# End of an FFN: splits of the embedding projection behind the last FFN tile, and half of that projection ahead of the norm's transposes

## Chip, core and metric

The kernel runs on one core of one Trainium2 chip. The metric is the device time of one execution in microseconds (us).

## What is computed

Two blocks in a row on 256 tokens of width 1024, in float32. The first block has an RWKV and a retention mixer and then a gated FFN with a short convolution; the second has a Mamba-style mixer, attention, and, behind each of these, a "per-layer embedding". The change sits where the first block's FFN ends and the second block begins. Cut to that, the reference is:

```python
def conv_ffn(h, w_up, conv_w, conv_b, w_down):
    u = h @ w_up
    ...
    u = sum(up[:, i:i + T] * conv_w[i] for i in range(CONV_WIDTH)) + conv_b
    gate, val = jnp.split(u, 2, axis=-1)
    return (jax.nn.gelu(gate, approximate=True) * val) @ w_down
...
    f = conv_ffn(rms_norm(h, norm_ffn_pre[l]), ffn_w_up[l], ffn_conv_w[l], ffn_conv_b[l], ffn_w_down[l])
    h = h + rms_norm(f, norm_ffn_post[l])
...
def mamba2_mixer(h, norm_w, in_w, ...):
    u = rms_norm_2(h, norm_w)
    zxbcdt = u @ in_w
...
def per_layer_embedding(h, p_i, norm_w, gate_w, proj_w):
    g = jax.nn.sigmoid((rms_norm_2(h, norm_w) @ gate_w).astype(jnp.float32))
    return (g * (p_i @ proj_w).astype(jnp.float32)).astype(h.dtype)
```

`p_i @ proj_w` doesn't depend on `h`. The kernel computes it early, once at each end of the FFN (index 0 ahead of it, index 1 behind it), and parks the result in DRAM (`ppd`) until the gates need it.

## The kernel before

Tokens lie in two halves of 128 (t = 0, 1). Every large product is done with three matmuls: each operand is split into a rounded part "hi" and a rest "lo", and hi*hi, hi*lo and lo*hi are summed in PSUM (`mm3`, `gemm_a` at line 273). The split (line 251) is one copy on ScalarE (hi, line 252) and one subtraction on VectorE (lo, line 253).

Weights come through `Stream.next` (line 218): SyncE issues a load of 512 KB into one of three `raw` buffers (line 230), then the chunk is split into buffers of a tag: `w`, `l`, `e` or `d`. A raw buffer is free when both halves of its split are done. Stream tiles are `whi/wlo`, `lhi/llo`, `ehi/elo`, `dhi/dlo` in the rows.

The FFN loop has 22 tiles of 128 features. For tile f TensorE computes gate and value (48 matmuls), then ScalarE and VectorE run the convolution (lines 980 and 983), the tanh form of the GELU (1002 to 1006) and the split of the result into `fah` and `fal`. The down projection of a tile follows two tiles later; for the last 7 tiles it is put off: the weights are split and kept, and `down_late` (833) does these products, 84 matmuls for both token halves, behind the last up projection. For t = 0 it takes five tiles of half 0, then two of half 1, then the last two of half 0; for t = 1 the other five of half 1. The sums stand in four `sm` banks.

Behind each half `post_norm_T` (927) follows: mean square (ScalarE Square at 921, GpSimd power at 294), the residual sum, a second mean square, the scaling (940), eight TensorE transposes (283) and the split of the transposed rows into `xTh`, `xTl`. They feed `gate_block` (1048), the z gate of the next mixer, whose weights are the four first chunks of `w_z` with tag `l`; it does half 0 and then half 1, 24 matmuls each.

`Proj` (296) is the embedding projection: its constructor loads and splits `pT` (256 KB) and two chunks of `w_proj` with tag `e`; `run(t, o)` does two groups of 6 matmuls (512 columns each), copies both to one `xs` buffer of 1024 columns (line 311, two such buffers, shared with the norms and the z gate) and stores it with one DMA (312).

A scheduler lays out the queue of each engine from the traced order and from when operands are ready by its own estimate of times; each engine then works through its queue in order. `tc.issue_after(ins)` puts every instruction traced inside the block on the engine of `ins` behind `ins` in that engine's queue. It adds no semaphore.

Of the kernel before, what the change touches and what calls it, by code (L numbers as in the profile page):

```python
# [15 lines left out]
AF = mybir.ActivationFunctionType  # L16
# [4 lines left out]
P = 128  # L21
T = 256
# [99 lines left out]
def tile_block(ctx: ExitStack, tc: tile.TileContext, io):  # L122
    nc = tc.nc
    V, S, G, PE = nc.vector, nc.scalar, nc.gpsimd, nc.tensor
    mult, add, sub = ALU.mult, ALU.add, ALU.subtract

    def pool(name, stack=ctx, **kw):
        return stack.enter_context(tc.tile_pool(name=name, bufs=1, reuse_waits="tile", **kw))
# [27 lines left out]
    def tl(pl, shape, tag, bufs=1, dt=F32):  # L156
        return pl.tile(shape, dt, tag=tag, name=tag, bufs=bufs)

    def mm():
        return tl(qp, [P, 512], "mm", 4)  # L160

    def sm():
        return tl(qp, [P, 512], "sm", 4)

    dp = pool("scratch", space=bass.MemoryType.DRAM)
    ppd = tl(dp, [4, P, D], "ppd")
# [84 lines left out]
    def split(hi, lo, src, eng=None):  # L251
        first = S.activation(out=hi, in_=src, func=AF.Copy)  # L252
        last_split[:] = first.ins, (eng or V).tensor_tensor(out=lo, in0=src, in1=hi.bitcast(F32), op=sub).ins  # L253

    def mm3(out, sh, sl, mh, ml, start, stop):
        PE.matmul(out, sh, mh, start=start, stop=False)  # L256
        PE.matmul(out, sh, ml, start=False, stop=False)  # L257
        return PE.matmul(out, sl, mh, start=False, stop=stop).ins  # L258

    def gemm_b(out, w, xT, nk=KD, off=0, start=True, stop=True, k0=0):  # L260

        for k in range(nk):
            c = slice(off + k * P, off + (k + 1) * P)
            mm3(out, w[0][:, c], w[1][:, c], xT[0][:, k0 + k, :], xT[1][:, k0 + k, :],
                start and k == 0, stop and k == nk - 1)
# [7 lines left out]
    def gemm_a(out, w, xT, t, k, off, start, stop, n=512):  # L273

        tk, c = slice(t * P, (t + 1) * P), slice(off, off + n)
        return mm3(out, xT[0][:, k, tk], xT[1][:, k, tk], w[0][:, c], w[1][:, c], start, stop)

    def transposes(src, n, xT, t, k0=0, ps_=None):

        for j in range(0, n, 4):  # L280
            ps = (ps_ or sm)().rearrange("p (a l) -> p a l", a=4)
            for i in range(4):
                last = PE.transpose(ps[:, i, :], src[:, (j + i) * P:(j + i + 1) * P], ident)  # L283
            d = (slice(None), slice(k0 + j, k0 + j + 4), slice(t * P, (t + 1) * P))
            split(xT[0][d], xT[1][d], ps)
        return last.ins

    last_split = []
# [7 lines left out]
    class Proj:  # L296
# [5 lines left out]
            st = Stream(io["w_proj"][i:i + 1], (tag,))  # L302
            self.ws = [st.next(), st.next()]

        def run(self, t, o):
            for b in range(2):
                ps = mm()
                c = slice(b * 512, (b + 1) * 512)
                for k in range(2):
                    gemm_a(ps, self.ws[k], self.px, t, k, b * 512, k == 0, k == 1)  # L310
                S.activation(out=o[:, c], in_=ps, func=AF.Copy)
            nc.sync.dma_start(out=ppd[2 * self.i + t], in_=o)


    ph = ExitStack()
# [5 lines left out]
    def b4(shape=(P, 1024)):  # L321
        return tl(p1, list(shape), "b4", 3)

    xT = (tl(p1, [P, KD, T], "xTh", 1, F32R), tl(p1, [P, KD, T], "xTl", 1, F32R))
# [8 lines left out]
    made = G.affine_select(out=ident, in_=ident, pattern=[[-1, P]], compare_op=ALU.is_ge, fill=0.0, base=0,  # L333
                           channel_multiplier=1).ins
# [8 lines left out]
    for t in range(2):  # L343
# [15 lines left out]
        for b in range(2):  # L359
            c = slice(b * 512, (b + 1) * 512)  # L360
# [436 lines left out]
    def halves(ps):  # L797
        return ps[:, 0:T], ps[:, T:2 * T]
# [57 lines left out]
    acc = None  # L856
    late = []
    pend = None
    for f in range(KD + 1):
# [24 lines left out]
        if pend is not None:  # L884
            k, x = pend
            if acc is None:
                acc = [[sm(), sm()], [sm(), sm()]]
# [13 lines left out]
    def rows(src, n=D):  # L901
        r = tl(late_pool, [P, D], "row", 2)[:, :n]
        nc.gpsimd.dma_start(out=r, in_=src.partition_broadcast(P))
        return r

    def xs_t():
        return tl(late_pool, [P, D], "xs", 2)

    def new_xT():
        return tl(late_pool, [P, KD, T], "xTh2", 1, F32R), tl(late_pool, [P, KD, T], "xTl2", 1, F32R)  # L910

    def halved(v):
        return [v[:, 0:512], v[:, 512:1024]]
# [3 lines left out]
    def mean_square(srcs, tag):  # L917

        ms = small([P, 2], tag)
        for b in range(2):  # L920
            S.activation(out=junk[b], in_=srcs[b], func=AF.Square, scale=1.0 / 32.0, accum_out=ms[:, b:b + 1])
        r = small([P, 1], tag + "r")
        V.tensor_scalar(out=r, in0=ms[:, 0:1], scalar1=ms[:, 1:2], scalar2=RMS_EPS, op0=add, op1=add)
        rsqrt(r, r, None)
        return r

    def post_norm_T(acc, gpost, gpre, xT, t):

        xs, h = halved(xs_t()), halved(h_t[t])
        gpost, gpre = halved(gpost), halved(gpre)  # L930
        r = mean_square(acc[t], "msa")
        for b in range(2):
            V.tensor_tensor(out=xs[b], in0=acc[t][b], in1=gpost[b], op=mult)
        for b in range(2):
            V.scalar_tensor_tensor(out=h[b], in0=xs[b], scalar=r, in1=h[b], op0=mult, op1=add)
        r = mean_square(h, "msb")
        for b in range(2):
            V.tensor_tensor(out=xs[b], in0=h[b], in1=gpre[b], op=mult)
        for b in range(2):
            scaled = V.tensor_scalar(out=xs[b], in0=xs[b], scalar1=r, scalar2=None, op0=mult)  # L940
            last = transposes(xs[b], 4, xT, t, 4 * b)
        return scaled.ins, last
# [19 lines left out]
    p2 = pool("p2", ph)  # L962
    wtags["e"] = (pool("p2e", ph), 3)
    wtags["d"] = (pool("p2d", ph), 4)
    proj = Proj(0, "e")
    xT = new_xT()
    gpost, gpre = rows(io["norms"][1]), rows(io["norms"][2])
    after = [post_norm_T(acc, gpost, gpre, xT, t) for t in range(2)]
    proj.run(0, xs_t())
    with tc.issue_after(after[0][1]):  # L970
        proj.run(1, xs_t())
    with tc.issue_after(opened):
        V.tensor_scalar(out=PR("fcw").rearrange("p (i f) -> p i f", i=3)[:, :, NF:], in0=PR("fcw").rearrange("p (i f) -> p i f", i=3)[:, :, NF:],
                        scalar1=0.5, scalar2=None, op0=mult)
# [2 lines left out]
    def conv(ps, c, wname, bname, ntap, nf, i):  # L977

        wv, bv = PR(wname), PR(bname)
        S.activation(out=c, in_=ps, func=AF.Identity, scale=wv[:, (ntap - 1) * nf + i:(ntap - 1) * nf + i + 1], bias=bv[:, i:i + 1])  # L980
        for d in range(1, ntap):
            j = (ntap - 1 - d) * nf + i
            V.scalar_tensor_tensor(out=c[:, d:], in0=ps[:, :T - d], scalar=wv[:, j:j + 1], in1=c[:, d:], op0=mult, op1=add)  # L983

    w_up, w_dn = Stream(io["w_up"], ("w", "w", "w", "e", "e", "e")), Stream(io["w_down"], ("l",) * 18 + ("d",) * 4)
    acc = [[sm(), sm()], [sm(), sm()]]
# [4 lines left out]
    for f in range(NF + LAG2):  # L991
        if f < NF:
            ps = mm()
            pg_, pv_ = halves(ps)
            for g_ in (pg_, pv_):
                gemm_b(g_, first.pop(0) if first else w_up.next(), xT)
            c = tl(p2, [P, 2, T], "fc", 3)
            conv(pg_, c[:, 0, :], "fcw", "fcb", 3, 2 * NF, f)
            conv(pv_, c[:, 1, :], "fcw", "fcb", 3, 2 * NF, NF + f)
            g_, v_ = c[:, 0, :], c[:, 1, :]  # L1000
            q_ = tl(p2, [P, T], "fq", 3)
            S.activation(out=q_, in_=g_, func=AF.Square, scale=math.sqrt(0.044715))
            V.scalar_tensor_tensor(out=q_, in0=q_, scalar=1.0, in1=g_, op0=add, op1=mult)
            S.activation(out=q_, in_=q_, func=AF.Tanh, scale=math.sqrt(2.0 / math.pi))
            V.scalar_tensor_tensor(out=g_, in0=q_, scalar=1.0, in1=g_, op0=add, op1=mult)
            V.tensor_tensor(out=g_, in0=g_, in1=v_, op=mult)
            a_ = tl(p2, [P, T], "fah", LATE2 + LAG2 + 1, F32R), tl(p2, [P, T], "fal", LATE2 + LAG2 + 1, F32R)
            split(a_[0], a_[1], g_)
        if f >= LAG2:
            k, x = f - LAG2, pend[f - LAG2]  # L1010
            w = w_dn.next()
            if k < NF - LATE2:
                down(acc, w, x, k, k == 0, False)
            else:
                late.append((w, x, False))
        if f < NF:
            pend.append(a_)
    proj = Proj(1, "e")


    xT = new_xT()
    gpost, gpre = rows(io["norms"][3]), rows(io["norms"][4])
    for t in range(2):
        down_late(acc, late, t, LT2, LT2T)
        post_norm_T(acc, gpost, gpre, xT, t)
    for t in range(2):
        proj.run(t, xs_t())
    ph.close()

    ph = ExitStack()  # L1030
# [33 lines left out]
    ps = mm()  # L1064
# [38 lines left out]
    ps = sm()  # L1103
# [35 lines left out]
    for c in range(2):  # L1139
        tk = slice(c * P, (c + 1) * P)  # L1140
        ps = sm()
# [6 lines left out]
    ps = sm()  # L1148
# [71 lines left out]
    acc = None  # L1220
# [17 lines left out]
    acc = [[mm(), mm()], [mm(), mm()]]  # L1238
# [5 lines left out]
    xT, g_ple = new_xT(), rows(io["norms"][5])  # L1244
# [41 lines left out]
    gate, xT = Gate(0, xT), new_xT2()  # L1286
# [99 lines left out]
    for t in range(2):  # L1386
        last = block(wkv, kvo[t], t)
# [3 lines left out]
        last = block(wq0, qo[t], t)  # L1391
# [225 lines left out]
```

## Times and profile before

| | us |
|---|---|
| median of 3 runs | 905.34 (902.51 to 908.39) |
| profiled execution | 906.97 |
| its span | 905.3 |
| TensorE busy | 863.9 (95%) |
| VectorE busy | 655.6 (72%) |
| ScalarE busy | 515.3 (57%) |
| GpSimd busy | 59.6 (7%) |

The span runs from the first to the last instruction; the profiled execution's time is 1.67 us longer. All start times below count from the start of the span. PE is TensorE, DVE VectorE, ACT ScalarE, POOL GpSimd and SP SyncE. The mean granted TensorE clock of the execution is 0.992 of full speed.

### The profile page before, as it was taken

The page shows a single profiled execution, that of the slowest core. Times are in us where ns is not written, and L with a number is a line of the kernel's source. Part 1 is how long each engine was busy: PE and PEld are TensorE (multiplying, and loading weights), DVE is VectorE, ACT ScalarE, POOL GpSimd, SP SyncE. Part 2 cuts the span into 40 slices and gives each one's busy share as a digit, 9 for nine tenths or more (in the row PEclk, how much of TensorE's full clock was granted, in tenths as well). Part 3 has the DMA queues.
Part 4 walks back from the last instruction along what each step waited for, and adds up shares of the span by engine and source line. Part 5 has one row for each costly group of instructions (what it writes and reads, how often), then busy time and mean ns, then how long its engine had stood idle before and what let it go on. Part 6 is the DMA issues. An engine that isn't in the chain of part 4 may idle for free.

```text
span 905.3 us, 15879 instructions
## 1 busy us (share of the span) xinstructions
PE 863.9 (95%) x6226; PEld 754.9 (83%) x6226; DVE 655.6 (72%) x1138; ACT 515.3 (57%) x917; POOL 59.6 (7%) x76
## 2 busy tenths in 40 slices
PE   9999999999999999999998999998999998899997
PEld 6788788789999799999997799887888777778776
DVE  7778856874665878888888767987774587757564
ACT  6555533454553666656666557677674465565652
POOL 2000000100000100000000102011000010101000
PEclk9999999999999999999999999999999999999999
DMA  8432442234765676655654627644343655432341
GB/s 279 145 131 97 135 132 71 96 115 140 241 202 175 182 246 230 221 173 183 206 190 153 228 92 242 202 167 163 119 161 95 198 174 165 155 124 95 115 139 48
DMA packets 42252, 145.48 MB, mean 161 GB/s; under 512 B 4993, under 2 KB 5569, under 8 KB 42178
## 3 DMA queue, kind: packets, MB, share of 16 engines
q1 hardware_dynamic: 41312, 141.32, 47.1%
q0 software_dynamic: 864, 3.15, 1.3%
q8 instruction: 49, 0.80, 0.4%
q14 instruction: 25, 0.20, 0.1%
q10 hardware_dynamic: 2, 0.00, 0.0%
HBM read 141.28 MB, written 3.18 MB: 160 GB/s over the span
## 4 chain that ended last, share of the span: by engine, by line
PE 42%; DMA 19%; DVE 15%; issue 14%; ACT 9%; POOL 2%; POOLq 0%; SPq 0%; ACTq 0%; DVEq 0%
PE mm L258 9%; PE mm L256 9%; PE mm L257 9%; DMA raw<-in_w_down 7%; DVE wlo L253 3%; DMA raw<-in_w_up 3%; PE sm L596 2%; ACT lhi L252 2%; ACT whi L252 2%; DMA raw<-in_w_ai 2%; PE sm L283 2%; DVE llo L253 2%; DVE elo L253 1%; DMA raw<-in_w_br 1%; PE sm L1198 1%
## 5 line engine op out<-in xcount | busy, mean ns | idle before, releaser
L252 ACT ACTIVATE whi<-raw 128x1024 fp32r<-128x1024 f32 (+1 forms) x131 | 134.4, 1030 | 111.6 <-PE mm L257 36.1
L253 DVE TENSOR_TENSOR wlo<-raw,whi 128x1024 fp32r<-128x1024 f32 (+1 forms) x130 | 153.8, 1188 | 58.7 <-ACT whi L252 57.8
L256 PE MATMUL mm<-xTh,whi 128*128 128x256 f32 x616 | 177.3, 288 | 0.2 <-ACT xTh L252 0.2
L257 PE MATMUL mm<-xTl,whi 128*128 128x256 f32 x616 | 176.2, 286 | 0.3 <-DVE xTl L253 0.3
L258 PE MATMUL mm<-xTh,wlo 128*128 128x256 f32 x616 | 175.9, 286 | 0.4 <-DVE wlo L253 0.4
L257 PEld LDWEIGHTS mm<-xTl,whi 128*128 128x128 f32 x616 | 119.1, 193 | 2.4 <-issue 0.7
L256 PEld LDWEIGHTS mm<-xTh,whi 128*128 128x128 f32 x616 | 118.9, 193 | 2.4 <-ACT xTh L252 0.5
L258 PEld LDWEIGHTS mm<-xTh,wlo 128*128 128x128 f32 x616 | 118.9, 193 | 1.2 <-DVE wlo L253 0.9
L253 DVE TENSOR_TENSOR llo<-raw,lhi 128x1024 fp32r<-128x1024 f32 x46 | 56.1, 1221 | 18.4 <-ACT lhi L252 17.9
L256 PE MATMUL mm<-whi,xTh 128*128 128x512 f32 x168 | 68.9, 410 | 0.0
L258 PE MATMUL mm<-whi,xTl 128*128 128x512 f32 x168 | 67.7, 403 | 0.0
L252 ACT ACTIVATE lhi<-raw 128x1024 fp32r<-128x1024 f32 x46 | 48.6, 1059 | 32.8 <-DMA raw<-in_w_down 13.3
L257 PE MATMUL mm<-wlo,xTh 128*128 128x512 f32 x168 | 67.1, 400 | 0.0
L256 PE MATMUL mm<-lhi,xTh 128*128 128x512 f32 (+1 forms) x156 | 61.2, 392 | 1.9 <-DVE cv L983 1.9
L257 PE MATMUL mm<-llo,xTh 128*128 128x512 f32 (+1 forms) x156 | 60.7, 389 | 0.0
L258 PE MATMUL mm<-lhi,xTl 128*128 128x512 f32 (+1 forms) x156 | 59.8, 384 | 0.0
L983 DVE SCALAR_TENSOR_TENSOR fc<-mm,par,fc 128x255 f32<-128x255 f32 x88 | 41.9, 478 | 7.8 <-ACT fc L980 7.3
L258 PE MATMUL mm<-xTh,elo 128*128 128x256 f32 x168 | 47.6, 283 | 0.0
L257 PE MATMUL mm<-xTl,ehi 128*128 128x256 f32 x168 | 47.6, 283 | 0.0
L256 PE MATMUL mm<-xTh,ehi 128*128 128x256 f32 x168 | 47.5, 283 | 0.0
L983 DVE SCALAR_TENSOR_TENSOR cv<-mm,par,cv 128x255 f32<-128x255 f32 (+2 forms) x72 | 34.2, 475 | 5.8 <-ACT cv L980 5.2
L258 PEld LDWEIGHTS mm<-whi,xTl 128*128 128x128 f32 x168 | 32.0, 191 | 6.8 <-DVE xTl L253 0.2
(468 smaller groups left out, 1977.4 us busy)
## 6 DMA issues: line engine op xcount, KB each, us to landing
raw<-in_w_up SPq DMA_DIRECT2D x44, 512.0 KB, 3.9
raw<-in_w_xbc SPq DMA_DIRECT2D x25, 512.0 KB, 4.3
raw<-in_w_ret SPq DMA_DIRECT2D x24, 512.0 KB, 3.7
raw<-in_w_down SPq DMA_DIRECT2D x22, 512.0 KB, 4.4
raw<-in_w_gate SPq DMA_DIRECT2D x16, 512.0 KB, 3.4
raw<-in_w_z SPq DMA_DIRECT2D x16, 512.0 KB, 4.2
raw<-in_w_so SPq DMA_DIRECT2D x16, 512.0 KB, 3.8
raw<-in_w_pg SPq DMA_DIRECT2D x16, 512.0 KB, 4.2
```

The costliest lines, as they stand in the source:

```text
L252: first = S.activation(out=hi, in_=src, func=AF.Copy)
L253: last_split[:] = first.ins, (eng or V).tensor_tensor(out=lo, in0=src, in1=hi.bitcast(F32), op=sub).ins
L256: PE.matmul(out, sh, mh, start=start, stop=False)
L257: PE.matmul(out, sh, ml, start=False, stop=False)
L258: return PE.matmul(out, sl, mh, start=False, stop=stop).ins
L283: last = PE.transpose(ps[:, i, :], src[:, (j + i) * P:(j + i + 1) * P], ident)
L596: PE.matmul(fv(px)[u, f, :], lhsT(f, x), rhs[u, f, :], start=True, stop=True)
L983: V.scalar_tensor_tensor(out=c[:, d:], in0=ps[:, :T - d], scalar=wv[:, j:j + 1], in1=c[:, d:], op0=mult, op1=add)
L1198: PE.matmul(py[:, i * 64:(i + 1) * 64], sg[:, i, :], x[:, i * 64:(i + 1) * 64], start=False, stop=i % 2 == 1)
```

## The change

`Proj.run` copies each group of 512 columns into a buffer of its own, one of the three `fc` buffers that the FFN tiles use for the convolution, stores it with a DMA of its own, and returns its last matmul. This holds at both ends of the FFN. Behind the FFN, the splits of `pT` and `w_proj` are queued behind both instructions of the last FFN tile's split (`made`). Then half 0's transposes are queued behind `proj.run(0)`, `proj.run(1)` behind those transposes, and half 1's norm is traced last.

```diff
-        def run(self, t, o):
+        def run(self, t):
             for b in range(2):
-                ps = mm()
-                c = slice(b * 512, (b + 1) * 512)
+                ps, o = mm(), tl(p2, [P, 2, T], "fc", 3).rearrange("p a l -> p (a l)")
                 for k in range(2):
-                    gemm_a(ps, self.ws[k], self.px, t, k, b * 512, k == 0, k == 1)
-                S.activation(out=o[:, c], in_=ps, func=AF.Copy)
-            nc.sync.dma_start(out=ppd[2 * self.i + t], in_=o)
+                    last = gemm_a(ps, self.ws[k], self.px, t, k, b * 512, k == 0, k == 1)
+                S.activation(out=o, in_=ps, func=AF.Copy)
+                nc.sync.dma_start(out=ppd[2 * self.i + t, :, b * 512:(b + 1) * 512], in_=o)
+            return last
...
-    proj.run(0, xs_t())
+    proj.run(0)
     with tc.issue_after(after[0][1]):
-        proj.run(1, xs_t())
+        proj.run(1)
...
             split(a_[0], a_[1], g_)
+            made = list(last_split)
...
-    proj = Proj(1, "e")
+
+    with tc.issue_after(made[0]), tc.issue_after(made[1]):
+        proj = Proj(1, "e")
...
     for t in range(2):
         down_late(acc, late, t, LT2, LT2T)
-        post_norm_T(acc, gpost, gpre, xT, t)
-    for t in range(2):
-        proj.run(t, xs_t())
+    with tc.issue_after(proj.run(0)):
+        turned = post_norm_T(acc, gpost, gpre, xT, 0)[1]
+    with tc.issue_after(turned):
+        proj.run(1)
+    post_norm_T(acc, gpost, gpre, xT, 1)
     ph.close()
```

## Rows read from the trace of the kernel before

**Rows 1.** The page, busy time of each engine and its share of the span.

```profile
PE 863.9 (95%) x6226; PEld 754.9 (83%) x6226; DVE 655.6 (72%) x1138; ACT 515.3 (57%) x917; POOL 59.6 (7%) x76
```

**Rows 2.** Timeline of TensorE: start us, us, engine, line, operation, tiles, [idle before <-releaser].

```profile
480.76 0.40 PE L256 MATMUL sm<-lhi,fah 128*128 128x512 f32 x1
...
490.08 0.39 PE L258 MATMUL sm<-lhi,fal 128*128 128x512 f32 x1
491.48 0.50 PE L256 MATMUL sm<-dhi,fah 128*128 128x512 f32 x1 [1.01 <-ACT fah L252]
...
492.83 0.40 PE L258 MATMUL sm<-dhi,fal 128*128 128x512 f32 x1
494.56 0.50 PE L256 MATMUL sm<-dhi,fah 128*128 128x512 f32 x1 [1.33 <-ACT fah L252]
...
495.84 0.39 PE L258 MATMUL sm<-dhi,fal 128*128 128x512 f32 x1
...
501.75 0.39 PE L257 MATMUL sm<-dlo,fah 128*128 128x512 f32 x1
504.19 1.09 PE L283 MATMUL sm<-cst,xs 128*128 128x128 f32 x8 [2.05 <-DVE xs L940]
...
506.05 0.40 PE L256 MATMUL mm<-ehi 128*128 128x512 f32 x1
...
511.50 0.39 PE L256 MATMUL mm<-lhi,xTh 128*128 128x512 f32 x1
...
513.86 1.06 PE L283 MATMUL sm<-cst,xs 128*128 128x128 f32 x8
```

**Rows 3.** Waits of ScalarE, 476.9 to 494.6: who for whom, us, times, longest.

```profile
ACT ehi L252 <- DMA raw<-in_w_proj: 2.3, 2, 1.4
...
ACT lhi L252 <- DMA raw<-in_w_z: 1.5, 1, 1.5
```

**Rows 4.** Busy time in one stretch: its length, then each engine (instructions), clock, DMA.

```profile
479.10:495.00 15.90, 13.56 (x66) 10.64 (x64) 13.03 (x28) 8.37 (x16) 0.00 (x0) 1.00 0.55 176
```

**Rows 5.** Groups of VectorE, 479.1 to 495.0: count, busy us, mean ns, idle before.

```profile
L253 DVE TENSOR_TENSOR elo<-raw,ehi 128x1024 fp32r<-128x1024 f32 (+1 forms) x3 | 3.1, 1039 | 0.1
...
L253 DVE TENSOR_TENSOR llo<-raw,lhi 128x1024 fp32r<-128x1024 f32 x1 | 1.2, 1224 | 0.9 <-ACT lhi L252 0.9
```

**Rows 6.** Timeline of SyncE's queue, projection and z loads, one store (merged issues).

```profile
476.70 2.92 SPq L230 DMA_DIRECT2D raw<-in_w_proj  x2
481.34 7.30 SPq L230 DMA_DIRECT2D raw<-in_w_z  x4
...
509.60 0.33 SPq L312 DMA_DIRECT2D ppd<-xs  x1
```

**Rows 7.** Timeline of ScalarE behind the last FFN tile.

```profile
494.42 2.00 ACT L252 ACTIVATE lhi<-raw 128x1024 fp32r<-128x1024 f32 x2
496.32 0.57 ACT L921 ACTIVATE junk<-sm 128x512 bf16<-128x512 f32 x1
```

**Rows 8.** The page, DMA issues: count, KB each, us to landing.

```profile
raw<-in_w_z SPq DMA_DIRECT2D x16, 512.0 KB, 4.2
```

**Rows 9.** Timeline of GpSimd and of VectorE: the power, and a split beside it.

```profile
501.99 1.21 DVE L253 TENSOR_TENSOR llo<-raw,lhi 128x1024 fp32r<-128x1024 f32 x1
...
502.21 1.40 POOL L294 TENSOR_TENSOR sm_msbr<-sm_msbr,mhalf 128x1 f32<-128x1 f32 x1 [2.92 <-DVE sm_msbr L923]
507.72 0.55 POOL L294 TENSOR_TENSOR sm_msar<-sm_msar,mhalf 128x1 f32<-128x1 f32 x1 [4.11 <-DVE sm_msar L923]
```

**Rows 10.** Timelines of ScalarE and VectorE behind half 1's transposes.

```profile
514.64 1.08 ACT L311 ACTIVATE xs<-mm 128x512 f32<-128x512 f32 x2 [2.67 <-DMA ppd<-xs]
...
516.31 1.29 DVE L253 TENSOR_TENSOR xTl<-sm,xTh 128x512 fp32r<-128x512 f32 x2 [2.20 <-ACT xTh L252]
```

**Rows 11.** Timelines at the head of the FFN, ScalarE and TensorE.

```profile
308.82 1.08 ACT L311 ACTIVATE xs<-mm 128x512 f32<-128x512 f32 x2
...
310.83 1.09 PE L283 MATMUL sm<-cst,xs 128*128 128x128 f32 x8 [1.06 <-DVE xs L940]
```

## The prediction

> **What bounds the kernel now.** The page's list of engines comes first: TensorE is busy 95% of the span [rows 1], so the kernel ends when TensorE's stream ends, and only holes in that stream are worth anything. The next view is TensorE's timeline around the end of the FFN [rows 2]. The reader is to see an even beat: from the first late down matmul at 480.76 to the 42nd at 490.08 they start every 9.32/41 = 0.227 us. Then come three holes. The stream stops at 490.31 and goes on at 491.48 (1.17 us); stops at 493.06 and goes on at 494.56 (1.50); and stops at 501.98 and goes on at 504.19 (2.21). The first two wait for `fah`, the hi half of FFN tiles 20 and 21; the third waits for the normalised `xs` that the transposes read. Restarts cost a little too: the six matmuls after the first hole take 1.58 us and the six after the second 1.51, where six beats are 1.36, so 0.37 more.
>
> As a sum: from 480.76 to the first matmul of the z gate at 511.50 are 30.74 us. The work in it is 84 late down matmuls (7 tiles, 2 token halves, 2 column halves, 3 products) and 24 of the projection, 108 x 0.227 = 24.5, and eight transposes, 0.85: 25.4. The other 5.3 us are the holes, and that is all the change can win there.
>
> Why is `fah` late? TensorE had finished the up projection of tile 21 at 480.76, but its `fah` came at 494. ScalarE's waits in that stretch [rows 3] show that it stood for the loads of `w_proj` (2.3 us, longest 1.4) and `w_z` (1.5), with the conv, Square and Tanh of tiles 19 to 21 queued behind. VectorE was busy 13.03 of 15.9 us [rows 4], 3.1 of them on the three `elo` and 1.2 on one `llo` [rows 5].
>
> **The change part by part.** *Order of the splits.* The three hi copies of the projection (ScalarE) and its three lo subtractions (VectorE) now stand behind tile 21's own split. The `w_z` split follows with them, although no edge names it: there are three raw buffers, the three projection loads hold them until they are split, so the `w_z` loads, issued from 481.34 before [rows 6], come behind those splits. Out of VectorE's stretch go 3.1 + 1.2 = 4.3 us of work, out of ScalarE's 3.8 us of waits for loads and four copies. What is left for VectorE is 13.0 - 4.3 = 8.7 us from 479.1, so 487.8 with no idle time, and 489.6 if the 1.8 us in which it waited for something other than `lhi` stay. TensorE reaches tile 20 at 490.31 and tile 21 at 491.68. Both are made by then, with some 2 us to spare for the last one. Bounds: all of 1.17 + 1.50 + 0.37 = 3.0 us goes, or nothing, if the stretch is held by VectorE in some other way. I take 3.0, since the same rows name the cover that leaves.
>
> *Half of the projection ahead of the transposes.* `proj.run(0)`, 12 matmuls or 2.73 us, now stands before the transposes of token half 0. With the holes gone, token half 0's sums are done at 493.0, the other half's at 493.03 + 30 x 0.227 = 499.9, and the projection's half at 502.6. The norm of half 0 took 7.87 us from its first Square (496.32) [rows 7] to its transposes (504.19) [rows 2]; starting at 493.2 it is ready at 501.1. So the third hole, 2.2 us, closes with 1.5 to spare. The transposes come later against the sums, but nothing needs their result before the z gate: 502.6 + 0.85 + 2.73 for `proj.run(1)` gives 506.2 for its first matmul, against 511.50, the full 5.3.
>
> *What comes back.* The moved splits don't vanish: they now queue on ScalarE and VectorE beside both norms, and so do the `w_z` splits. The projection's are through by about 489.6 + 3.1 = 492.7. The first `w_z` load can start when the first raw buffer is free, about 490, and lands 4.2 us later [rows 8]; the fourth needs the first one's split, so it lands near 501. The four splits, 1.1 us each on either engine, then fall into half 0's norm, where one stood before. At worst three of them delay it: 3.3 less the 1.5 of slack is 1.8 us. Half 1's norm took 7.7 us from its last sum (506.2) to its transposes (513.86); from 499.9 it is ready at 507.6, and its split parts 3.7 us behind that (513.86 to 517.6 before [rows 10]), 511.3, while the z gate starts on half 1 at 506.2 + 24 x 0.227 + 0.85 = 512.5. A slack of 1.2 us, against perhaps two `wlo` splits and late ends of half 0's chain: at worst another 1.7. So 0 to 3.5 us come back; nothing below zero, as no work leaves either engine. I take 1.2, nearer to zero, because the scheduler orders by readiness, and the trace shows it putting the Square of half 0 straight behind its last sum.
>
> One of these delays can be read directly. GpSimd's power on one column took 0.55 us by itself and 1.40 us where a VectorE split started 0.2 us before it [rows 9]; 0.85 us more, in the middle of the chain. More splits beside four such powers make that likelier. The 1.2 hold one such stretch. The Trainium skill, "SBUF — State Buffer", section "Who interferes with whom", says that a VectorE instruction with two SBUF inputs contends with a GpSimd instruction that reads SBUF; the trace agrees (1.40 against 0.55 us). By that rule each of the four powers could be held, four times 0.85 less the one held before, 2.55 us ahead of the slack; this lies inside the bounds above.
>
> *Evictions in pieces of 512 columns, in `fc` instead of `xs`.* The same four copies of 0.54 us as before per layer; four DMA issues more in all, 0.33 us each on SyncE's queue [rows 6], ahead of raw loads that no hole of TensorE waits for here. What goes: ScalarE stood 2.67 us for a store from `xs` with the half 1 split behind it [rows 10], hidden by the z gate's first half. What comes: the fourth piece reuses the first one's `fc` buffer and waits for its store. At the first FFN two copies stand at 308.82, ahead of a hole of 1.06 us before half 1's transposes [rows 11]. There they may fall into the chain (two of 0.54: +1.1) or leave it shorter (-1.1); I take 0, as they wait behind the norm in program order.
>
> **Sum.** -3.0 - 2.2 + 1.2 = -4.0 us (0.4%). The profiled execution took 906.97 us (span 905.3 and 1.67 around it); it would take 903.0. It lay 1.63 above the median of 905.34, so the median goes to 901.3. Afterwards weights come at the pace at which buffers are freed, so the gain is carried to the end.
>
> **The rivals.**
> - *The gain is returned in the norms.* Splits fall in both chains at their worst: -5.2 + 3.5 = -1.7, 903.6. For it: VectorE is dense there and the power stretch has a row. Against: slack of 1.5 and 1.2 us. Chance 0.22.
> - *The change doesn't do what it says for `fah`.* VectorE itself holds tiles 20 and 21, and only the transposes' hole closes: -2.2 + 0.4, a third of the 1.2, 903.5. Against it: the idle time and the splits make up 7 of the 15.9 us. Chance 0.08.
> - *Slower: the `w_z` splits stand ahead of half 0's Square on ScalarE.* That engine works in order, so the norm would wait for the fourth `w_z` load, about 501, and start at 501.7; transposes 7.87 later, 509.6, is 7.0 us after TensorE gets there, against 5.2 won: +1.8, 907.1, and some 3 more if half 1's chain follows as late. It decides from a first Square at 499.9 on. For it: two `lhi` copies did stand right ahead of that Square [rows 7]. Chance 0.10.
> - *More than the holes*, through a better order downstream: below 897. Nothing in the rows speaks for it. Chance 0.05.
>
> **How the numbers follow.** The forecast has the other 0.55: 901.3, with its own range 898.5 to 903.5. The range reaches to the first two rivals and most of the third: 897.0 to 906.8. A measurement of this kernel tells about 1% from no change, 9 us; the holes hold 5.3, so faster by over 1% is 0.04, slower by over 1% (the third rival with more behind it, or a new wait later) 0.04, within 1% 0.92.
>
> **What would show it.** Right: no wait for `fah` in the late down matmuls; `ehi` copies after the last `fah`; `w_z` loads issued near 490 instead of 481; 12 projection matmuls directly ahead of half 0's transposes; the z gate's first matmul about 4 us earlier, near 507.5, and the span near 901.3. Wrong: a hole ahead of either norm's transposes of over 2 us, a wait of the z gate for `lhi`, or ScalarE idle on `w_z` ahead of a Square.

## The result and the profile after

| | before | after |
|---|---|---|
| median of 7 runs, us | 905.34 (902.51 to 908.39) | 912.19 (910.95 to 913.16) |
| profiled execution, us | 906.97 | 913.16 |
| its span, us | 905.3 | 911.4 |

The ratio of the medians is 1.0084, its 95% interval 1.0061 to 1.0106. The change costs 6.85 us; forecast were 4.0 us less, and 912.19 lies outside the range. That is within 1% of no change, but the interval leaves 1 out.

The engines' busy times first, from the page of the profile after:

```profile
PE 867.0 (95%) x6226; PEld 758.0 (83%) x6226; DVE 658.0 (72%) x1138; ACT 517.9 (57%) x917; POOL 57.7 (6%) x76
```

Against [rows 1] TensorE does as many matmuls and is busy 3.1 us longer. So the same work ran slower in places, and the rest of the 6.1 us of span is idle time. To find both, the execution is cut at TensorE instructions: the FFN's head goes from the first projection matmul to the first up matmul, the FFN to the last up matmul, the tail to the first z matmul, the z gate to its last matmul. These times are differences of starts in TensorE's timelines.

| us | head | FFN | tail | z gate | behind it |
|---|---|---|---|---|---|
| before | 8.96 | 168.46 | 30.86 | 11.69 | 382.08 |
| after | 15.07 | 169.83 | 33.26 | 11.58 | 378.88 |

The tail, which the change is about, is 2.4 us longer. The head, where only the projection's copies changed, is 6.1 us longer. The last column is 3.2 us shorter; over the twelve profiled executions of this study it lies between 373.7 and 382.1 and the FFN between 168.3 and 172.2, so in these two columns a few us between two single executions mean nothing.

**The head.** ScalarE's timeline of the kernel before, at the residual Squares (input `h`) of token half 0:

```profile
300.78 0.63 ACT L921 ACTIVATE junk<-h 128x512 bf16<-128x512 f32 x1 [1.25 <-DVE h L935]
...
302.36 0.61 ACT L921 ACTIVATE junk<-h 128x512 bf16<-128x512 f32 x1
```

The same place after, with VectorE's instructions that make `h`:

```profile
299.48 1.40 DVE L935 SCALAR_TENSOR_TENSOR h<-xs,sm_msar,h 128x512 f32<-128x512 f32 x2
...
305.27 0.60 ACT L310 ACTIVATE fc<-mm 128x512 f32<-128x512 f32 x1 [6.10 <-PE mm L258]
305.76 0.62 ACT L921 ACTIVATE junk<-h 128x512 bf16<-128x512 f32 x1
...
306.85 0.63 ACT L921 ACTIVATE junk<-h 128x512 bf16<-128x512 f32 x1
```

The copy of the projection's first 512 columns now stands ahead of the Square. ScalarE waits 6.10 us for matmuls that start at 302.75, and the Square behind it goes at 305.76 instead of 300.78, 5.0 us later. Its half of `h` was made by about 300.2, so it stood ready for some 5 of the 6.10 us. The Trainium skill, "PSUM — Partial Sum Buffer", section "Engine vs sequencer instructions", calls ScalarE's queue strictly first in, first out; the trace agrees: the ready Square didn't pass the waiting copy. Whether the other buffer or the smaller pieces moved the copy ahead was not separated. TensorE's timeline after shows what follows:

```profile
305.29 0.39 PE L258 MATMUL mm<-ehi,elo 128*128 128x512 f32 x1
310.02 1.97 PE L283 MATMUL sm<-cst,xs 128*128 128x128 f32 x8 [4.34 <-DVE xs L940]
...
312.21 0.63 PE L257 MATMUL mm<-elo,ehi 128*128 128x512 f32 x1
312.64 0.63 PE L258 MATMUL mm<-ehi,elo 128*128 128x512 f32 x1
...
316.24 1.04 PE L283 MATMUL sm<-cst,xs 128*128 128x128 f32 x8
```

One beat behind 305.29, at 305.52, TensorE has nothing left until 310.02: 4.5 us. Then it runs at half speed: the eight transposes take 1.97 us (1.09 in [rows 11]), and the next matmuls, up to 315.20, start 0.43 us apart where the beat (the time from one start to the next) is 0.227. From the transposes of half 0 to those of half 1 it is 6.22 us; at full speed 0.85 + 12 x 0.227 = 3.57, so 2.65 for the clock. 4.5 + 2.65, less the hole of 1.06 ahead of half 1 that is gone [rows 11], makes the 6.1.

**The tail.** TensorE's timeline after, to be held against [rows 2]:

```profile
506.61 0.39 PE L258 MATMUL sm<-dhi,fal 128*128 128x512 f32 x1
506.84 0.39 PE L256 MATMUL mm<-ehi 128*128 128x512 f32 x1
...
509.33 0.39 PE L258 MATMUL mm<-ehi,elo 128*128 128x512 f32 x1
514.62 1.97 PE L283 MATMUL sm<-cst,xs 128*128 128x128 f32 x8 [4.89 <-DVE xs L940]
...
520.91 0.40 PE L256 MATMUL mm<-lhi,xTh 128*128 128x512 f32 x1
```

The 84 late down matmuls run from 487.77 to 506.84 on the beat (19.07 = 84 x 0.227); no wait for `fah` is left. But the third hole, 2.21 us before, now goes from 509.56 to 514.62, 5.06 us. Behind it the clock has fallen again. The windows show it. Behind the length stand the busy times of PE, PEld (TensorE's weight loads), DVE, ACT and POOL, then the granted clock, the DMA engines' share and GB/s:

```profile
509.60:514.60 5.00, 0.12 (x1) 0.00 (x0) 4.56 (x8) 3.84 (x10) 1.40 (x1) 0.88 0.29 86
514.60:520.90 6.30, 6.28 (x20) 5.32 (x21) 6.30 (x11) 4.33 (x9) 1.65 (x3) 0.55 0.78 248
520.90:526.00 5.10, 5.10 (x28) 4.30 (x27) 4.13 (x8) 3.09 (x6) 1.40 (x1) 1.00 0.97 359
```

Where the clock reads 1.00 the engine is at its 2.4 GHz level. In the window from 514.60 it is at 0.55, that is nearly all the time at 1.2 GHz: from the transposes to the z gate 6.29 us pass, against 3.58 at full speed, 2.7 more. So the tail: -3.0 for `fah`, +2.85 for the third hole, +2.7 for the clock, +2.5; measured +2.4.

Why half 0's norm was late is read on ScalarE, behind the last FFN tile (compare [rows 7]):

```profile
496.12 0.42 ACT L252 ACTIVATE fah<-fc 128x256 fp32r<-128x256 f32 x1 [0.95 <-DVE fc L1006]
496.44 2.52 ACT L252 ACTIVATE ehi<-raw 128x512 fp32r<-128x512 f32 x3
501.61 1.06 ACT L252 ACTIVATE lhi<-raw 128x1024 fp32r<-128x1024 f32 x1 [2.65 <-DMA raw<-in_w_z]
504.83 1.06 ACT L252 ACTIVATE lhi<-raw 128x1024 fp32r<-128x1024 f32 x1 [2.16 <-DMA raw<-in_w_z]
505.80 0.58 ACT L921 ACTIVATE junk<-sm 128x512 bf16<-128x512 f32 x1
```

and on SyncE's queue (compare [rows 6]):

```profile
482.17 2.91 SPq L230 DMA_DIRECT2D raw<-in_w_proj  x2
497.81 6.47 SPq L230 DMA_DIRECT2D raw<-in_w_z  x4
```

Half 0's sums are complete at 487.77 + 54 x 0.227 = 500.0. Its Square starts at 505.80, behind two copies of z weights that wait for their loads. The loads are late since they get their raw buffers only when the projection is split: issued from 497.81, 16.5 us later than before, where the FFN's end itself moved by 7.0.

### The profile page after: what moved, and what is told of

Same layout as the page of the kernel before. It is cut to its first block, busy times and chain, and to the rows that moved or that the text cites. A ratio compares the mean times of both kernels' runs of the same rounds, so it can differ in the third digit from the quotient of the medians.

```text
span 911.4 us, 15890 instructions
## 1 busy us (share of the span) xinstructions
PE 867.0 (95%) x6226; PEld 758.0 (83%) x6226; DVE 658.0 (72%) x1138; ACT 517.9 (57%) x917; POOL 57.7 (6%) x76
## 4 chain that ended last, share of the span: by engine, by line
PE 50%; DMA 14%; issue 13%; DVE 13%; ACT 8%; POOL 2%; POOLq 0%; SPq 0%; ACTq 0%; DVEq 0%
PE mm L258 11%; PE mm L256 11%; PE mm L257 11%; DMA raw<-in_w_down 4%; PE sm L596 2%; DMA raw<-in_w_z 2%; DVE wlo L253 2%; DMA raw<-in_w_up 2%; PE sm L283 2%; PE sm L256 2%; ACT lhi L252 2%; PE sm L257 2%; PE sm L258 2%; DMA raw<-in_w_ai 2%; PE sm L1493 1%
## 5 line engine op out<-in xcount | busy, mean ns | idle before, releaser
L980 ACT ACTIVATE fc<-mm,par 128x256 f32<-128x256 f32 x44 | 24.4, 554 | 23.2 <-DVE fc L983 23.1
```

## The experiments

Theory: two waits in ScalarE's queue hold all of the loss. At the head the projection's copy ahead of the Square costs 6 us in place; at the tail the held-back splits make the z loads late, and their copies ahead of the Square cost the hole and the clock. Rival: the tail's new order on TensorE (half of the projection early) is what costs. The kernels ran in three groups, each with the kernel before beside it; its medians were 903.74 (beside the e kernels), 903.89 (f) and 902.64 (g), and each ratio is against the one beside it. All stage times are of one profiled execution each.

| us | median | ratio, 95% interval | head | tail | z gate |
|---|---|---|---|---|---|
| e1_head_whole | 907.46 | 1.0039, 1.0013 to 1.0064 | 8.96 | 34.81 | 11.89 |
| e2_tail_before | 907.36 | 1.0043, 1.0016 to 1.0071 | 14.96 | 27.32 | 11.70 |
| e3_head_behind_squares | 904.20 | 0.9998, 0.9978 to 1.0019 | 9.99 | 30.27 | 11.92 |
| e4_z_behind_square | 909.08 | 1.0061, 1.0040 to 1.0081 | 15.09 | 26.92 | 18.01 |
| f1_half_ahead_only | 904.48 | 1.0007, 0.9985 to 1.0030 | 8.96 | 28.16 | 14.49 |
| f2_splits_only | 907.38 | 1.0053, 1.0028 to 1.0078 | 8.96 | 36.01 | 11.58 |
| f3_fill | 917.04 | 1.0146, 1.0100 to 1.0193 | 14.16 | 35.48 | 12.35 |
| f6_z_behind_second | 901.66 | 0.9983, 0.9960 to 1.0005 | 8.96 | 25.54 | 16.29 |
| g1_late_turn | 905.53 | 1.0027, 1.0005 to 1.0048 | 8.96 | 25.55 | 19.89 |
| g2_late_turn_f1 | 900.66 | 0.9976, 0.9953 to 1.0000 | 8.96 | 28.02 | 13.35 |

**The two ends apart: e1 and e2.** e1 has the old `run` (here `run_whole`) at the head and the changed tail:

```diff
-    proj.run(0)
+    proj.run_whole(0, xs_t())
     with tc.issue_after(after[0][1]):
-        proj.run(1)
+        proj.run_whole(1, xs_t())
```

> The change, but ahead of the FFN the projection is evicted as in the kernel before (1024 columns of an xs buffer, one store for each token half); everything behind the FFN is as in the change. Theory (the loss sits at the head of the FFN, 15.07 us from the first projection matmul to the first up matmul against 8.96 before): 912.2 - 6.1 = 906.1 us, and that stretch back at 9.0 us with the granted clock at 1.00. Rival (the loss sits behind the FFN, the head's hole is made good later): 911 to 912 us.

e2 keeps the changed head and has the old tail:

```diff
-    with tc.issue_after(made[0]), tc.issue_after(made[1]):
-        proj = Proj(1, "e")
+    proj = Proj(1, "e")
...
-    with tc.issue_after(proj.run(0)):
-        turned = post_norm_T(acc, gpost, gpre, xT, 0)[1]
-    with tc.issue_after(turned):
-        proj.run(1)
-    post_norm_T(acc, gpost, gpre, xT, 1)
+        post_norm_T(acc, gpost, gpre, xT, t)
+    for t in range(2):
+        proj.run_whole(t, xs_t())
```

> The kernel before, but ahead of the FFN with the change's evictions in pieces; everything behind the FFN is as before. Theory (head): 905.3 + 6.1 = 911.4 us. Rival (loss behind the FFN): 905.3 us. If both parts cost on their own, this and the run with the whole eviction at the head add up to the change's 6.9 us.

Neither the theory nor the rival of these two came true: each end alone costs about half, +3.7 us (e1) and +3.6 (e2), together 7.3 against 6.85. The head comes back to 8.96 in e1 and stays at 14.96 in e2, so its 6 us are due to the copies. That e2 nevertheless loses only 3.6 fits its tail: 27.32 us, 3.5 under that of before, with no wait for `fah`. TensorE comes 6 us late, while loads, ScalarE and VectorE catch up; this gives part of the head's loss back. This is argued and not shown, since the profiled execution of e2 took 901.39 us, the shortest of its ten. TensorE's timeline of e1, whose tail is the longer one:

```profile
496.76 0.50 PE L256 MATMUL sm<-dhi,fah 128*128 128x512 f32 x1 [0.86 <-ACT fah L252]
...
514.17 1.97 PE L283 MATMUL sm<-cst,xs 128*128 128x128 f32 x8 [6.21 <-DVE xs L950]
```

Here a wait for `fah` is left, although the splits are held back.

**The head by queue order alone: e3.** The pieces stay, but their copies are queued behind the Squares (`squares` lists the last Square of each mean square, in the order in which they are traced):

```diff
-    proj.run(0)
-    with tc.issue_after(after[0][1]):
+    with tc.issue_after(squares[1]):
+        proj.run(0)
+    with tc.issue_after(after[0][1]), tc.issue_after(squares[3]):
         proj.run(1)
```

> The change, with one thing added ahead of the FFN: on ScalarE the pieces of token half 0 are queued behind the Squares of the residual of half 0, those of half 1 behind the Squares of half 1's residual. Pieces, buffers and stores stay. Theory (a copy that waits for TensorE stands ahead of a Square, so the norm stands still; the order is the cause): 906 us, ScalarE's wait of 6.1 us gone, TensorE's hole of 4.5 us down to the 1 to 2 us of the kernel before. Rival (the smaller stores, or the ring of three fc buffers, cost the time): 911 to 912 us.

ScalarE's timeline of e3 at the head, and TensorE's at the tail:

```profile
302.59 0.61 ACT L923 ACTIVATE junk<-h 128x512 bf16<-128x512 f32 x1
...
305.96 1.09 ACT L310 ACTIVATE fc<-mm 128x512 f32<-128x512 f32 x2 [1.52 <-PE mm L258]
```

```profile
508.11 1.71 PE L283 MATMUL sm<-cst,xs 128*128 128x128 f32 x8 [2.91 <-DVE xs L943]
```

Head 9.99, time 904.20: the same buffers and stores, without the loss. So the pieces are not dear; their place in the queue is. e3's tail (30.27) is also better than e1's (34.81) with the same tail code. By VectorE's timelines the last instruction that makes the last FFN tile started 6.5 us behind the last up matmul in e3, 12.0 in e1, 8.9 after. In e1, e3, f2, f3 and after, where z copies stand ahead of it, the first Square follows that instruction by 8.6 to 9.7 us, so a late tile makes a late norm. Why the tile varies so stays open, and with it how much of e3's 904.20 is the head and how much the tail alone costs: 3.7 us by e1, but little by e3.

**The two halves of the tail: f1 and f2**, both with e1's head. f1 takes the edges from the splits and keeps the new order on TensorE; f2 keeps the edges and has the old order:

```diff
-    with tc.issue_after(made[0]), tc.issue_after(made[1]):
-        proj = Proj(1, "e")
+    proj = Proj(1, "e")
```

```diff
-    with tc.issue_after(proj.run(0)):
-        turned = post_norm_T(acc, gpost, gpre, xT, 0)[1]
-    with tc.issue_after(turned):
-        proj.run(1)
-    post_norm_T(acc, gpost, gpre, xT, 1)
+        post_norm_T(acc, gpost, gpre, xT, t)
+    for t in range(2):
+        proj.run(t)
```

> Head of the FFN as in the kernel before (whole evictions). Behind the FFN only the order of TensorE's work is as in the change (half of the projection ahead of half 0's transposes, the other half behind them, in pieces); the projection's splits are not held back behind the last FFN tile. Theory (the projection's half fills the third hole of 2.2 us, and the held-back splits are what cost the time): the two holes for fah stay (2.7 us), the third one closes, the z gate's first matmul comes about 2 us earlier than before, the time is 2 us under the kernel before of the same call. Rival (the later transposes and the pieces' copies cost as much as the hole): equal to before or above it.

> Head of the FFN as in the kernel before. Behind the FFN only the projection's splits are held back behind the last FFN tile; the norms and the projection stand as before (pieces of 512 columns). Theory (held-back splits hold the three raw buffers, so the w_z loads start about 16 us later than before and their copies wait ahead of the first Square): no hole for fah, a hole of 5 us or more ahead of half 0's transposes with the clock down behind it, 3 to 4 us above the kernel before, as in the run with the whole eviction at the head. Rival (half of the projection ahead of the transposes is what costs): equal to before.

TensorE's timeline of f2:

```profile
510.36 1.97 PE L283 MATMUL sm<-cst,xs 128*128 128x128 f32 x8 [7.49 <-DVE xs L950]
```

The held-back splits alone make the hole, 7.49 us, and cost 3.5 us; f1 costs 0.6, nothing that can be told. The rival, that TensorE's new order costs the time, falls. But f1 doesn't win the 2 us that its own theory gave it either, and its trace shows why: its tail is 2.7 us shorter than before and its z gate 2.8 longer. The first two lines, of TensorE in f1, are the waits for `fah`, which stay; the third stands in the z gate:

```profile
491.29 0.50 PE L256 MATMUL sm<-dhi,fah 128*128 128x512 f32 x1 [0.61 <-ACT fah L252]
...
494.38 0.50 PE L256 MATMUL sm<-dhi,fah 128*128 128x512 f32 x1 [1.37 <-ACT fah L252]
...
513.00 1.10 PE L283 MATMUL sm<-cst,xs 128*128 128x128 f32 x8 [1.83 <-DVE xs L950]
```

TensorE reaches half 1's transposes earlier, and half 1's norm is not earlier.

**The z copies behind the Squares: e4 and f6.** e4 is the change with the z gate's weights queued behind half 0's first two Squares; f6 has e1's head and puts them behind its second two:

```diff
-    for _ in gate_block(0, "tile"):
-        pass
+    with tc.issue_after(squares[4]):
+        for _ in gate_block(0, "tile"):
+            pass
```

```diff
+    with tc.issue_after(squares[5]):
+        for _ in gate_block(0, "tile"):
+            pass
```

> The change, with one thing added behind the FFN: all ScalarE work of the first z gate, the four hi copies of w_z among it, is queued behind the two Squares of half 0's sums. Theory (two copies that wait 2.7 and 2.2 us for w_z loads stand ahead of the first Square, which comes at 505.8 with the sums done at 500.0): the first Square follows the sums within 0.5 us, the hole ahead of half 0's transposes falls from 5.1 to 2 or 3 us (two copies now stand ahead of the second pair of Squares), the clock stays up: about 908 us. Rival (VectorE's subtractions and the stretched power make the norm late): hole still about 5 us, 911 to 912 us.

> Head as in the kernel before, behind the FFN as in the change, but all ScalarE work of the first z gate, its hi copies of w_z among it, is queued behind the second pair of Squares of half 0. Theory (the copies' waits ahead of Squares are all that is wrong with the tail): the hole ahead of half 0's transposes is under 1 us, the stretch from the last up matmul through the z gate is 40 us or less, against 42.8 before: 902 us or less. Rival (the seven splits and the late loads have no room in this stretch at all; moved from half 0's norm they hold half 1's norm or the z gate): 44 us or more for that stretch, 906 us or more.

ScalarE and then TensorE of e4:

```profile
498.83 0.60 ACT L923 ACTIVATE junk<-sm 128x512 bf16<-128x512 f32 x1 [0.30 <-PE sm L258]
...
504.97 1.06 ACT L252 ACTIVATE lhi<-raw 128x1024 fp32r<-128x1024 f32 x1 [3.09 <-DMA raw<-in_w_z]
505.94 0.61 ACT L923 ACTIVATE junk<-h 128x512 bf16<-128x512 f32 x1
```

```profile
509.62 1.09 PE L283 MATMUL sm<-cst,xs 128*128 128x128 f32 x8 [0.63 <-DVE xs L943]
...
518.62 1.97 PE L283 MATMUL sm<-cst,xs 128*128 128x128 f32 x8 [1.83 <-DVE xs L943]
```

The first Square now stands right behind its sum, and the hole of 5.06 us shrinks to a wait of 0.63. But the next z copy, waiting 3.09 us, holds the second pair, and the loss turns up in the z gate (18.01). f6 takes these out too. TensorE of f6:

```profile
503.15 1.03 PE L283 MATMUL sm<-cst,xs 128*128 128x128 f32 x8
...
512.30 1.68 PE L283 MATMUL sm<-cst,xs 128*128 128x128 f32 x8 [2.20 <-DVE xs L953]
```

Half 0's transposes wait for nothing and the tail is 25.54 us, the 5.3 under before that the forecast hoped for. Against e1, from which only this edge differs, the time, each taken against the kernel before beside it, goes from 3.7 us above to 2.2 below. e4 and f6 show the tail's mechanism: with the copies out of the way the hole is gone. The size is less sure, as e3, without this edge, lies only 0.5 above. Some 4.6 of the 5.3 us go again in the z gate, at half 1's transposes; tail and z gate take 41.8 us, where 40 or less was expected.

**The clock: f3.** The change, with 20 matmuls that add nothing to the result between `proj.run(0)` and the transposes:

```diff
+    ran, spare_ps = proj.run(0), mm()
+    with tc.issue_after(ran):
+        for _ in range(20):
+            ran = PE.matmul(spare_ps, proj.px[0][:, 0, 0:P], proj.ws[0][0][:, 0:512], start=True, stop=True).ins
+    with tc.issue_after(ran):
-    with tc.issue_after(proj.run(0)):
```

> The change with 20 extra matmuls (128x512, into a spare PSUM bank that nothing reads) between the projection's first half and half 0's transposes, 4.5 us at the full clock, so that TensorE works through the hole of 5.1 us. Theory (behind a hole in which TensorE stands still the granted clock goes to 1.2 GHz, and eight transposes and nine matmuls at that level cost 2.6 us): the granted clock behind the hole stays at 2.4 GHz, the stretch from the last up matmul to the z gate falls from 33.3 to 30.7 us, the time to 909.6. Rival (the clock falls there for another reason, or the extra work itself delays): the clock falls all the same, 912.

TensorE of f3:

```profile
510.79 4.70 PE L1031 MATMUL mm<-ehi 128*128 128x512 f32 x20
515.93 1.09 PE L283 MATMUL sm<-cst,xs 128*128 128x128 f32 x8 [0.45 <-DVE xs L940]
...
523.51 1.10 PE L283 MATMUL sm<-cst,xs 128*128 128x128 f32 x8 [3.74 <-DVE xs L940]
```

In that stretch the fill does what was expected: transposes 1.09 instead of 1.97 us, the projection on its full beat, and the window behind the fill has the clock at 1.00:

```profile
515.90:519.60 3.70, 3.67 (x20) 3.00 (x20) 3.70 (x8) 2.67 (x6) 1.12 (x2) 1.00 0.82 216
```

So the half clock behind the hole came from the idle time and not from the work that follows. The time did not follow: 917.04, where 909.6 was expected. The scheduler put half 1's transposes ahead of the z gate, where they make a new hole of 3.74 us, and behind them the z matmuls start 0.43 us apart. Tail and z gate are 3.0 us longer than after; the rest of the loss wasn't located.

**Half 1's transposes later: g1 and g2.** g1 is f6 and g2 is f1, with half 1's transposes behind the z gate's half 0 (24 matmuls). The edit is that of g2; in g1 the new block stands inside the edge of f6:

```diff
-            last = transposes(xs[b], 4, xT, t, 4 * b)
+            last = transposes(xs[b], 4, xT, t, 4 * b) if turn else xs
...
-    post_norm_T(acc, gpost, gpre, xT, 1)
+    xs1 = post_norm_T(acc, gpost, gpre, xT, 1, False)[1]
...
+    zblock = gate_block(0, "tile")
+    for _ in range(4):
+        last = next(zblock)
+    with tc.issue_after(last):
+        for b in range(2):
+            transposes(xs1[b], 4, xT, 1, 4 * b)
+    for _ in zblock:
+        pass
```

> This is f6_z_behind_second (head evictions ahead of TensorE's transposes as in the kernel before, the changed tail, the z gate's ScalarE work behind half 0's second Squares) with half 1's eight transposes put on TensorE behind the z gate's half 0 instead of inside it. Theory (what the tail wins is lost again as long as TensorE meets half 1's transposes before their input is made): in f6 that place was a wait of 2.20 us with the half clock behind it (z gate 16.52 us against 11.92 before), so here the wait is under 0.6 us, the z gate takes 12 to 13.5 us, tail and z gate together 38.5 to 40 us against 42.06, and the time is 898 to 900.5, 1 to 3.5 us under f6's 901.7. Rival (the wait only moves on, to the second half's z matmuls, which need the transposes' copies): z gate 15.5 to 17 us with a wait of 1.5 to 2.5 us ahead of z half 1, time 901 to 903.

> This is f1_half_ahead_only (only the order on TensorE changed at the tail: half of the projection ahead of the transposes; splits not held back; head evictions as in the kernel before) with half 1's eight transposes behind the z gate's half 0. Theory: f1's z gate of 14.72 us loses the 1.83 us wait ahead of half 1's transposes and comes to 12 to 13 us, tail and z gate to 40 to 41 us against 42.88, time 901.5 to 902.5, some 2 us under f1's 904.5. Rival (the wait only moves on to z half 1): z gate 14 to 15 us, time 904 to 905, no gain.

ScalarE and TensorE of g1:

```profile
520.11 1.06 ACT L252 ACTIVATE whi<-raw 128x1024 fp32r<-128x1024 f32 x1 [6.05 <-DMA raw<-in_w_xbc]
...
522.13 1.07 ACT L252 ACTIVATE xTh<-sm 128x512 fp32r<-128x512 f32 x2
```

```profile
515.96 1.03 PE L283 MATMUL sm<-cst,xs 128*128 128x128 f32 x8
522.77 0.80 PE L256 MATMUL mm<-lhi,xTh 128*128 128x512 f32 x1 [5.78 <-ACT xTh L252]
```

In g1 the transposes wait for nothing, and yet the rival came true, with a longer wait than it named: the copy of their result stands behind a copy of the next weights, which waits 6.05 us for a load. TensorE waits 5.78, and from 522.70 to 527.50 the granted clock is 0.53. It is the third place with the same pattern. In g2, whose loads are not late, the wait is gone:

```profile
514.27 1.03 PE L283 MATMUL sm<-cst,xs 128*128 128x128 f32 x8
515.60 0.50 PE L256 MATMUL mm<-lhi,xTh 128*128 128x512 f32 x1 [0.30 <-ACT xTh L252]
```

z gate 13.35 against f1's 14.49, and 900.66 us, 2.0 under the kernel before beside it, where f1 was 0.6 above. The interval ends at 1.0000: the best version of the study, but not shown to be faster than before. Raw buffers of the z gate's own, which would uncouple its loads from the projection's splits, weren't tried.

## Why the prediction was wrong

- **TensorE's holes as the whole budget, 5.3 us**: right. f6, with no hole left in the tail, has 25.54 us against 30.86.
- **Order of the splits, -3.0**: the mechanism was right, the close size partly luck. Tile 21 was forecast made at 489.6, 9.0 us behind the last up matmul at 480.64; here it was done 9.3 behind it (496.99), and all waits for `fah` went. With the head as before, f2, f6 and g1 (splits held back) have no wait for `fah` either, and f1 and g2 (not held back) keep both. But the same tail code made the tile between 6.5 and 12.0 us behind, with a wait of 0.86 left in e1, and in e2 the waits went without any edge, behind the late head. So the late head may have helped here too.
- **Half of the projection ahead, -2.2**: wrong in this kernel. The chain behind it was to start with the Square at 493.2, 12.6 us behind the last up matmul. It started 18.15 behind, and the hole grew by 2.85 instead of closing. Where it did close, half 1's norm failed the forecast: ready at 507.6, 27.0 behind the last up matmul, was worked out, with a slack of 1.2 us; its transposes waited until 31.1 behind in f6 and 32.2 in f1, and the z gate was 4.6 and 2.8 us longer.
- **What comes back, 1.2 of at most 3.5**: mis-sized, and the reason given for the low end ("the scheduler orders by readiness") is what failed. That the z loads would come late was worked out there (issue near 490; measured 497.81, less 7.0 is 490.8; first landing 494.2, its copy started at 501.61, less 7.0 is 494.6), but not that two of their copies would keep their place ahead of the Square. In the tail 7.6 us came back (-5.2 became +2.4): 5.06 of hole and 2.7 for the clock, to 0.2. Two of the four powers of both norms were held, 1.40 us each, where the term had one.
- **Evictions in pieces, 0**: the step that failed worst. "I take 0, as they wait behind the norm in program order": the first copy stood ahead of the Square, and ScalarE waited 6.10 us for TensorE. The upper bound, +1.1, was the price of the copies' own duration; the price of the wait in front of one was not looked for. Measured: 6.1 us in the head (15.07 against 8.96 before and in e1), and 3.1 (the change less e1) to 3.6 (e2) in the median.
- **The rival "z splits ahead of half 0's Square"**, chance 0.10, is what happened at the tail. It was to decide from a first Square at 499.9, that is 19.3 us behind the last up matmul; it came at 18.15 and cost nevertheless, since two terms were missing. The norm took 8.82 us to the transposes (505.80 to 514.62), not 7.87, and the clock took 2.7. Two copies stood ahead, not all four.
- **No price for the clock** stood anywhere in the sum. Two holes of 4.5 and 5.06 us each cost a further 2.7 us behind them.

## What to carry to other kernels

When a producer's copy out of PSUM is given another buffer or cut in pieces, its place in the engine's in-order queue is a new cost: list what is queued behind it and price the wait in front of it, not its own duration. Holding back splits also holds back every load that shares their buffers, and the copies of those loads may stand ahead of a norm. A hole closed ahead of one token half is worth only what the other half's chain allows, and a long hole is priced with the slow stretch behind it (2.7 us here, behind 4.5 and 5.06).

## What the runs showed of the hardware that was not expected

What a fall of the clock costs: the eight transposes take up to 1.97 us instead of 1.03 to 1.09, and 512-column matmuls start 0.43 us apart. It came behind waits of 4.34 and 4.89 us (after), 7.49 (f2, transposes 1.97), 6.21 (e1, 1.97), 2.91 (e3, 1.71) and 3.74 (f3, transposes still 1.10, the matmuls behind them slow). Shorter waits went both ways: full speed behind the 2.05 of before [rows 2] and 1.83 in f1 (transposes 1.10), but the lower level behind 2.20 in f6 (1.68) and behind 1.83 in e4 (1.97), which follows waits of 0.37 at 513.84 and 1.25 at 515.82. At the head of e3 a wait of 2.08 was followed by transposes of 1.09 us and then, from 314.0 to 317.2, by a granted clock of 0.50. The window of f6 behind its wait:

```profile
512.30:518.00 5.70, 5.70 (x22) 4.87 (x23) 3.20 (x5) 2.63 (x5) 0.00 (x0) 0.70 0.92 351
```

TensorE is busy all of it and the clock reads 0.70. So the length of the last wait alone doesn't tell whether the clock falls.

GpSimd's power was held longer than in [rows 9]. GpSimd and VectorE of f6:

```profile
509.76 1.97 POOL L294 TENSOR_TENSOR sm_msbr<-sm_msbr,mhalf 128x1 f32<-128x1 f32 x1
```

```profile
508.95 2.35 DVE L253 TENSOR_TENSOR llo<-raw,lhi 128x1024 fp32r<-128x1024 f32 x2
```

It ends at 511.73, behind the end of the two splits at 511.30; g1 has the same 1.97. With no VectorE instruction beside it the power takes 0.55 (f6, at 499.91), beside one split 1.40 [rows 9]. The rule of the Trainium skill, "SBUF — State Buffer", section "Who interferes with whom", that a VectorE instruction with two SBUF inputs contends with a GpSimd instruction that reads SBUF, fits these three. But two in a row need not both hold it. GpSimd and VectorE of the kernel before:

```profile
511.76 0.84 POOL L294 TENSOR_TENSOR sm_msbr<-sm_msbr,mhalf 128x1 f32<-128x1 f32 x1
```

```profile
510.97 2.34 DVE L253 TENSOR_TENSOR wlo<-raw,whi 128x1024 fp32r<-128x1024 f32 x2
```

Here the power ends at 512.60, 0.7 us ahead of the end of the second split. What decides it stays open.
